# Windowed attention: softmax rows divided on GpSimd, transposed in place, one more stage between the steps

## The chip, the cores and the metric

One NeuronCore of a Trainium2 chip runs the whole program. The metric is the device time of one execution in microseconds (us), the median of several runs. Five engines work side by side, each through its own queue in order: TensorE (PE in the rows; PEld is its weight load), VectorE (DVE), ScalarE (ACT), GpSimd (POOL) and SyncE (SP), which issues the weight loads. Engines wait for each other through semaphores.

## The reference, cut to what matters

The program is two layers of a transformer-like block on 256 latent and 256 context tokens of width 1024. The change lies in the first layer, between the input projection and the output projection, where attention runs:

```python
def window_attention(q, k, v, k_ctx, v_ctx, sink):
    ...
    s_loc = jnp.where(valid[None, :, None, None], s_loc, NEG_INF)
    ...
    m = jnp.maximum(jnp.maximum(jnp.max(s_loc, axis=-1, keepdims=True),
                                jnp.max(s_ctx, axis=-1, keepdims=True)), s_sink)
    p_loc = jnp.exp(s_loc - m)
    p_ctx = jnp.exp(s_ctx - m)
    inv = 1.0 / (jnp.sum(p_loc, axis=-1, keepdims=True) + jnp.sum(p_ctx, axis=-1, keepdims=True)
                 + jnp.exp(s_sink - m))
    o = jnp.einsum('bnkgqs,bnskd->bnqkgd', (p_loc * inv).astype(v.dtype), vw) \
        + jnp.einsum('bnkgql,blkd->bnqkgd', (p_ctx * inv).astype(v.dtype), v_ctx)
```

`s_loc` and `s_ctx` are the scaled products of queries with keys, `valid` the band. There are 8 query heads and 2 key/value heads of width 64. Context queries read context keys only. The factor `inv` is one number per query row and head.

## The kernel before

All large products run in three passes of a split float format (`mm3`, L335 to L338): each fp32 operand is cut into a high part, cast by ScalarE (`wh`, L126), and a low part, subtracted by VectorE (`wl`, L127). A `Stream` object holds the weights in the order in which they are used: 1 MB units go through four raw buffers (`pump_dma`, issued on SP at L112), and `pump` cuts them in halves into four pairs of `wh`/`wl` buffers as these come free.

The program text gives each engine's instructions a priority by position. A planner of the framework then sets the order of each engine's queue by a model of durations, before anything runs. `issue_after` puts an instruction behind another one on the same engine.

The modulation vector of the layer is computed in 12 pieces (`ada_step(n)`): two 1 MB units, 16 small matmuls (`ada_mm`, L430), a copy, and one step later `ada_fin`: four transposes (L451), or, for pieces 4, 5, 10 and 11, products that spread a gate over 128 rows (L446, one for each of two streams) with a copy of each (L447).

Attention runs over 16 pairs (c, t): c counts four pairs of query heads, t four blocks of 128 queries. Blocks with t below 2 are latent (512 keys), the others context (256 keys). So four pairs, one value of c, are a period, with two long and two short pairs. For each pair j:

- `scores(j)`: for both heads a product with the high part of the keys (L929) and one with the low part (L932), and for long pairs a product that adds the mask from `CE` through the identity (L937, fp32). A pair takes two of the four `mm` banks of PSUM.
- `soft(j)`: VectorE row maxima (L947), the negative shift (L948), ScalarE exponentials with row sums (L953), the sink's term (L949, L956), the sum (L957) and its reciprocal (L958).
- `ptrans(j)`: TensorE turns the exponentials in blocks of 128 (L968) into the two `tr` banks, and ScalarE copies them out (L970).
- `av(j)`: the products with the values (L983) into one `po` bank, and products of the reciprocal, spread over 64 columns, with the identity (L987, fp32) into the other `po` bank. At the end of a period ScalarE copies that second bank (L992), VectorE multiplies (L993), and the result is cut into parts (L994, L995).

The loop at L999 issues `scores(j)`, `soft(j)`, `ptrans(j-1)`, `av(j-2)`, and between them `cut_q` (splitting the next query heads, L905, L906) and `sgu` (splitting the other half of the output projection's input, L916, L917). Weight splits for the output projection (`woe`) may be issued whenever buffers are free. After the loop the output projection uses all eight banks, then comes the residual, a norm (L564, L603) and the dense feed-forward layer, in which `Side` sums the second layer's modulation on VectorE (L498, L500).

## Time and profile before

| | us |
|---|---|
| median of 3 runs | 1601.19 (1600.59 to 1602.11) |
| the profiled execution, its own time | 1600.52 |
| its span in the trace | 1598.7 |
| PE busy | 1551.5 (97%) |
| DVE busy | 1286.8 (80%) |
| ACT busy | 981.1 (61%) |
| POOL busy | 0.2 (0%) |

The profile is one execution. Busy shares are averages over stages with different limits; matmuls overlap in the pipeline and their ends are modelled, so the time that a group of matmuls takes is best read from its start to the start of the next one.

### The profile page before, as it was taken

Reading aid. Unit: us, or ns where it says so; the run is one execution under the profiler, and the core shown is the slowest. Engines: PE = TensorE matmul, PEld = TensorE weight load, DVE = VectorE, ACT = ScalarE, POOL = GpSimd, SP = SyncE. Lnnn points to the kernel's source line nnn. Section 1 sums busy time; section 2 is a strip of 40 time slices with the busy share of each in tenths; the row PEclk is TensorE's granted clock in tenths of the full one; section 3 lists DMA queues with packets and bytes.
Section 4 is the critical chain, followed back from the end, with each engine's and each line's share of the span. In section 5 each row is a group of like instructions: output and inputs, shape, how many; then the busy total and the mean of one; then the engine's idle time right before and its main releaser. Section 6 shows DMA issues by size and latency. Waiting matters only on the chain.

```text
span 1598.7 us, 20230 instructions
## 1 busy us (share of the span) xinstructions
PE 1551.5 (97%) x7518; PEld 1237.4 (77%) x7518; DVE 1286.8 (80%) x1817; ACT 981.1 (61%) x1292; POOL 0.2 (0%) x4
## 2 busy tenths in 40 slices
PE   5999999999999999999999999999999999999996
PEld 3775787888888887776578888888888888888885
DVE  3577557475877576599899998998989899898987
ACT  4435625322222224679688877887778777877775
POOL 0000000000000000000000000000000000000000
PEclk9999999999999999999999999999999999999998
DMA  8867143444536441414699989999999999999980
GB/s 296 284 220 241 49 134 106 158 134 156 193 124 211 156 142 57 132 53 164 213 358 352 378 325 370 322 380 354 363 363 330 369 364 367 336 346 367 365 303 29
DMA packets 204267, 398.22 MB, mean 249 GB/s; under 512 B 7930, under 2 KB 66552, under 8 KB 204160
## 3 DMA queue, kind: packets, MB, share of 16 engines
q1 hardware_dynamic: 201184, 395.34, 69.7%
q10 hardware_dynamic: 2976, 1.50, 0.4%
q8 instruction: 61, 1.00, 0.3%
q14 instruction: 46, 0.38, 0.1%
HBM read 395.76 MB, written 1.05 MB: 248 GB/s over the span
## 4 chain that ended last, share of the span: by engine, by line
PE 87%; DVE 8%; ACT 2%; DMA 2%; issue 1%; ACTq 0%; DVEq 0%
PE mm L337 18%; PE mm L336 18%; PE mm L338 18%; PE po L337 8%; PE po L338 8%; PE po L336 8%; PE po L430 1%; PE tr L1441 1%; DVE wl L127 1%; PE po L983 1%; PE tr L1381 1%; PE tr L968 1%; DVE xn L500 1%; DMA raw<-in_w_in_e_dram 1%; DMA raw<-in_ada_w_o_dram 1%
## 5 line engine op out<-in xcount | busy, mean ns | idle before, releaser
L126 ACT CAST wh<-raw 128x1024 fp32r<-128x1024 f32 (+1 forms) x644 | 662.5, 1046 | 447.0 <-PE mm L337 145.4
L127 DVE TENSOR_TENSOR wl<-raw,wh 128x1024 fp32r<-128x1024 f32 (+1 forms) x644 | 759.4, 1214 | 127.5 <-ACT wh L126 115.9
L338 PE MATMUL mm<-wh,hLa 128*128 128x512 f32 (+1 forms) x800 | 299.2, 374 | 0.1
L337 PE MATMUL mm<-wl,xTH 128*128 128x512 f32 (+1 forms) x768 | 289.9, 377 | 0.0
L336 PE MATMUL mm<-wh,xTH 128*128 128x512 f32 (+1 forms) x768 | 287.3, 374 | 0.9 <-DVE xTH L1402 0.9
L336 PE MATMUL mm<-hH,wh 128*128 128x512 f32 (+1 forms) x608 | 228.7, 378 | 1.7 <-ACT gT L1148 1.5
L338 PE MATMUL mm<-hH,wl 128*128 128x512 f32 (+1 forms) x608 | 224.8, 371 | 0.5 <-DVE wl L127 0.5
L338 PEld LDWEIGHTS mm<-wh,hLa 128*128 128x128 f32 x800 | 150.9, 189 | 26.4 <-DVE hLa L1405 1.3
L337 PEld LDWEIGHTS mm<-wl,xTH 128*128 128x128 f32 x768 | 144.8, 189 | 27.1 <-DVE wl L127 3.0
L336 PEld LDWEIGHTS mm<-wh,xTH 128*128 128x128 f32 x768 | 144.8, 188 | 26.5 <-DVE xTH L1402 1.5
L337 PE MATMUL po<-wl,mg 128*128 128x512 f32 x352 | 137.4, 390 | 0.0
L338 PE MATMUL po<-wh,mg 128*128 128x512 f32 x352 | 136.4, 390 | 0.0
L336 PEld LDWEIGHTS mm<-hH,wh 128*128 128x128 f32 x608 | 114.2, 189 | 24.0 <-issue 2.0
L338 PEld LDWEIGHTS mm<-hH,wl 128*128 128x128 f32 x608 | 114.5, 188 | 20.1 <-DVE wl L127 0.7
L336 PE MATMUL po<-wh,mg 128*128 128x512 f32 x352 | 128.9, 391 | 0.0
L337 PE MATMUL mm<-hLb,wh 128*128 128x512 f32 (+1 forms) x304 | 112.9, 372 | 0.6 <-DVE hLb L616 0.6
L337 PE MATMUL mm<-hLa,wh 128*128 128x512 f32 (+1 forms) x304 | 112.8, 371 | 0.5 <-DVE hLa L616 0.5
L500 DVE SCALAR_TENSOR_TENSOR xn<-raw,act,xn 128x512 f32<-128x512 f32 x112 | 81.7, 747 | 1.2
L337 PEld LDWEIGHTS po<-wl,mg 128*128 128x128 f32 x352 | 66.2, 188 | 13.8 <-DVE wl L127 0.4
L336 PEld LDWEIGHTS po<-wh,mg 128*128 128x128 f32 x352 | 66.2, 188 | 13.5
L338 PEld LDWEIGHTS po<-wh,mg 128*128 128x128 f32 x352 | 66.0, 188 | 13.5
L337 PE MATMUL po<-wl,gH 128*128 128x512 f32 x176 | 69.9, 397 | 0.0
(392 smaller groups left out, 1873.9 us busy)
## 6 DMA issues: line engine op xcount, KB each, us to landing
raw<-in_moe_w_dram SPq DMA_DIRECT2D x264, 1024.0 KB
raw<-in_ffn_w_dram SPq DMA_DIRECT2D x33, 1024.0 KB
raw<-in_ada_w_e_dram SPq DMA_DIRECT2D x24, 1024.0 KB
raw<-in_ada_w_o_dram SPq DMA_DIRECT2D x24, 1024.0 KB
raw<-in_w_in_o_dram SPq DMA_DIRECT2D x10, 1024.0 KB
raw<-in_w_in_e_dram SPq DMA_DIRECT2D x7, 1024.0 KB
raw<-in_w_out_o_dram SPq DMA_DIRECT2D x5, 1024.0 KB
raw<-in_w_out_e_dram SPq DMA_DIRECT2D x2, 1024.0 KB
```

The lines of the kernel that those rows point to most:

```text
L126: sp = (self.nc.scalar.copy(hv, src), self.nc.vector.tensor_tensor(lv, src, hv.bitcast(F32), op=ALU.subtract))
L127: self.nc.vector.tensor_tensor(lv, src, hv.bitcast(F32), op=ALU.subtract))
L336: T.matmul(dst, aH, bH, start=start, stop=False)
L337: T.matmul(dst, aH, bL, start=False, stop=False)
L338: return T.matmul(dst, aL, bH, start=False, stop=stop)
L430: T.matmul(p[32 * g:32 * g + 32, :], act[:, 4 * u + g, :], w[:, g, :], start=(u == 0), stop=(u == 1))
L500: V.scalar_tensor_tensor(acc[s_], w[:, k, :], c, acc[s_], op0=ALU.mult, op1=ALU.add)
L968: T.transpose(p[:, P * b:P * b + P], pr[:, P * b:P * b + P], ident)
L983: T.matmul(ob[c][0][64 * i:64 * i + 64, P * t:P * t + P], vv[:, b, 64 * i:64 * i + 64], pts[i][:, P * jj:P * jj + P], start=(jj == 0), sto ...
L1381: T.matmul(p[:, 256 * j:256 * j + n], h[:, i, cs], dsp(i), start=(x == 0 and j == 0), stop=(x == 3 and j == 1))
L1441: T.transpose(p[:, P * j:P * j + P], s1[:, P * j:P * j + P], ident)
```

## The change

Each row of exponentials is multiplied by its reciprocal on GpSimd, in place, before it is transposed; the transposed blocks are copied back over the same tile; and the products that spread the reciprocal, and what follows them, are gone. `ptrans` and `av` of a pair come one iteration later (j-2 and j-3). The tag `pt` has eight buffers in place of six, and the query rotation's scratch tile is one of them. The mask and a copy of the identity are turned into the one-pass format by GpSimd, and the mask product uses them. Of the query splits, the copies of heads c = 1 to 3 move to GpSimd, and `sgu` moves to GpSimd whole. Pieces 8 and 9 of the modulation come after the query products, 10 and 11 in iterations 1 and 7; the units of piece 8 are loaded after the last query unit. Between piece 8 and the end of the loop, weights are split only in iterations 8, 10, 12 and 14, one half each.

```diff
         self.behind = None
+        self.hold = False

...

     def pump(self, n=None):
         self.pump_dma()
+        if self.hold and n is None:
+            return
         end = len(self.halves) if n is None else self.n_split + n
         while self.n_split < end:
             i, j = self.halves[self.n_split]
...
         ada_units("ae", we, n)
     for i, un in enumerate(e1_units):
         units.append(un)
-        for n in ((1, 3), (4,), (5,), (6,), (7,), (8,), (9, 10, 11), ())[i]:
+        for n in ((1, 3), (4,), (5,), (6,), (7,), (), (8, 9, 10, 11), ())[i]:
             ada_units("ae", we, n)
     units.append(kunit(("woe", 1), a["w_out_e"][0], 2, 2, 0, D))
     units += [woe_unit(u) for u in range(2)]
...
             pin.enter_context(tc.issue_after(last.ins))
             nc.scalar.dma_start(selb, a["shape_consts"][:, C_SELB:C_MASK])
             nc.scalar.dma_start(LT, a["shape_consts"][:, C_LT:C_SELB])
-            CE = sp.tile([P, C_ID - C_MASK], F32, name="CE")
-            nc.scalar.dma_start(CE, a["shape_consts"][:, C_MASK:C_ID])
-            cos, sin = CE[:, C_COS - C_MASK:C_COS - C_MASK + 256], CE[:, C_SIN - C_MASK:C_SIN - C_MASK + 256]
-            sw = sp.tile([P, 512], F32, tag="pt", bufs=6, name="sw").rearrange("p (g q) -> p g q", g=4)
+            CE = sp.tile([P, C_ID - C_COS], F32, name="CE")
+            nc.scalar.dma_start(CE, a["shape_consts"][:, C_COS:C_ID])
+            cos, sin = CE[:, 0:256], CE[:, 256:512]
+            mask = cpA.tile([P, 512], F32, tag="rtmp", bufs=2, name="mask")[:, 0:256]
+            nc.scalar.dma_start(mask, a["shape_consts"][:, C_MASK:C_COS])
+            masks = cpA.tile([P, 512], F32R, tag="rtmp", bufs=2, name="masks")
+            maskR, identR = masks[:, 0:256], masks[:, 256:384]
+            nc.gpsimd.tensor_copy(maskR, mask)
+            nc.gpsimd.tensor_copy(identR, ident)
+            sw = sp.tile([P, 512], F32, tag="pt", bufs=8, name="sw").rearrange("p (g q) -> p g q", g=4)
             nc.scalar.dma_start(sw, a["sgu_w"][0].rearrange("g p q -> p g q"))
             sb = sp.tile([P, 4, P], F32, tag="sb", name="sb")
             nc.scalar.dma_start(sb.rearrange("p g q -> p (g q)"), bcast_row(a["sgu_b"][0], 512))
...
                     for k in range(2):
                         mm3(pq[c], wH[:, k, cs], wL[:, k, cs], hH[:, 2 * u + k, :], hL[:, 2 * u + k, :],
                             u == 0 and k == 0, u == 3 and k == 1)
-                if u % 2 == 1:
-                    ada_step(8 + u // 2)
-            ada_fin(*pend.pop())
+            st.hold = True
+            for n in (8, 9):
+                ada_step(n)
             QS = [big("xn", [P, 4, 512], F32R), sp.tile([P, 4, 512], F32R, tag="vg", name="QS1")]
             qs = {}

             def rope_q(c):
-                qs[c] = ht() if c in (1, 2) else sp.tile([P, 512], F32, tag="pt", bufs=6, name=nm("q"))
+                qs[c] = ht() if c in (1, 2) else sp.tile([P, 512], F32, tag="pt", bufs=8, name=nm("q"))
                 rope(qs[c], pq[c])

             def cut_q(c):
                 q = qs.pop(c)
                 for i in range(2):
                     me, ot = slice(64 * i, 64 * i + 64), slice(64 - 64 * i, 128 - 64 * i)
-                    S.copy(QS[i][me, c], q[me, :])
+                    (S.copy if c == 0 else nc.gpsimd.tensor_copy)(QS[i][me, c], q[me, :])
                     V.tensor_tensor(QS[i][ot, c], q[me, :], QS[i][me, c].bitcast(F32), op=ALU.subtract)
             rope_q(0)
             cut_q(0)
             for c in range(1, 4):
                 rope_q(c)
-            ada_step(10)
-            pend.append(("ae", 11, ada_mm("ae", 11)))
             xH, xL = hH, hL

             def sgu(g):
-                S.copy(xH[:, g, :], uT[:, g, :])
-                V.tensor_tensor(xL[:, g, :], uT[:, g, :], xH[:, g, :].bitcast(F32), op=ALU.subtract)
+                nc.gpsimd.tensor_copy(xH[:, g, :], uT[:, g, :])
+                nc.gpsimd.tensor_tensor(xL[:, g, :], uT[:, g, :], xH[:, g, :].bitcast(F32), op=ALU.subtract)

             pairs = [(c, t) for c in range(4) for t in range(NT)]
-            sc_t, pr_t, ri_t, pt_t, ob = {}, {}, {}, {}, {}
+            last_n, sc_t, pr_t, ob = {}, {}, {}, {}

             def scores(j):

...
                 if t < 2:
                     off = P - P * t
                     for i in range(2):
-                        T.matmul(ps[i][:, off:off + P], ident, CE[:, P * t:P * t + P], start=False, stop=True)
+                        T.matmul(ps[i][:, off:off + P], identR, maskR[:, P * t:P * t + P], start=False, stop=True)
                 sc_t[j] = ps

             def soft(j):
...
                 V.tensor_tensor(snk, sk[:, :, c], neg, op=ALU.add)
                 prs = []
                 for i in range(2):
-                    pr = sp.tile([P, 512], F32, tag="pt", bufs=6, name=nm("pr"))
+                    pr = sp.tile([P, 512], F32, tag="pt", bufs=8, name=nm("pr"))
                     S.activation(pr[:, :n], ps[i][:, :n], AF.Exp, bias=neg[:, i:i + 1], scale=0.125,
                                  accum_out=sums[:, i:i + 1])
                     prs.append(pr)
                 S.activation(snk, snk, AF.Exp)
                 V.tensor_tensor(sums, sums, snk, op=ALU.add)
                 V.reciprocal(sums, sums)
+                for i in range(2):
+                    last_n[j] = nc.gpsimd.tensor_scalar(prs[i][:, :n], prs[i][:, :n], sums[:, i:i + 1], None, op0=ALU.mult)
                 pr_t[j] = prs
-                ri_t[j] = sums

             def ptrans(j):
+
                 nb = 4 if pairs[j][1] < 2 else 2
-                pts = []
-                for pr in pr_t.pop(j):
+                for pr in pr_t[j]:
                     p = tr()
                     for b in range(nb):
                         T.transpose(p[:, P * b:P * b + P], pr[:, P * b:P * b + P], ident)
-                    pt = sp.tile([P, 512], F32, tag="pt", bufs=6, name=nm("pt"))
-                    S.copy(pt[:, :P * nb], p[:, :P * nb])
-                    pts.append(pt)
-                pt_t[j] = pts
+                    S.copy(pr[:, :P * nb], p[:, :P * nb])

             def av(j):
                 c, t = pairs[j]
-                pts = pt_t.pop(j)
+                pts = pr_t.pop(j)
                 if c not in ob:
-                    ob[c] = po(), po()
+                    ob[c] = po()
                 blocks = range(4) if t < 2 else range(2, 4)
                 nb = len(blocks)
                 for jj, b in enumerate(blocks):
                     for i in range(2):
-                        T.matmul(ob[c][0][64 * i:64 * i + 64, P * t:P * t + P], vv[:, b, 64 * i:64 * i + 64],
+                        T.matmul(ob[c][64 * i:64 * i + 64, P * t:P * t + P], vv[:, b, 64 * i:64 * i + 64],
                                  pts[i][:, P * jj:P * jj + P], start=(jj == 0), stop=(jj == nb - 1))
-                ri = ri_t.pop(j)
-                for i in range(2):
-                    T.matmul(ob[c][1][64 * i:64 * i + 64, P * t:P * t + P], ri[:, i:i + 1].to_broadcast([P, 64]), ident,
-                             start=True, stop=True)
                 if t == NT - 1:
-                    o, r = ob.pop(c)
-                    q = sp.tile([P, 512], F32, tag="pt", bufs=6, name=nm("o"))
-                    S.copy(q, r)
-                    V.tensor_tensor(q, o, q, op=ALU.mult)
-                    last_o[0] = S.copy(xH[:, 4 + c, :], q)
-                    V.tensor_tensor(xL[:, 4 + c, :], q, xH[:, 4 + c, :].bitcast(F32), op=ALU.subtract)
+                    o = ob.pop(c)
+                    last_o[0] = S.copy(xH[:, 4 + c, :], o)
+                    V.tensor_tensor(xL[:, 4 + c, :], o, xH[:, 4 + c, :].bitcast(F32), op=ALU.subtract)

             NCB = len(pairs)
             last_o = [None]
-            for j in range(NCB + 2):
+            for j in range(NCB + 3):
                 if j < NCB:
                     scores(j)
                     soft(j)
-                if j % 4 == 1 and j < 12:
-                    cut_q(j // 4 + 1)
-                if 1 <= j <= NCB:
-                    ptrans(j - 1)
-                if 2 <= j:
-                    av(j - 2)
-                if j % 4 == 2 and j < NCB:
-                    sgu(j // 4)
+                if j == 1:
+                    cut_q(1)
+                if j in (4, 5):
+                    with tc.issue_after(last_n[j - 2].ins):
+                        cut_q(j - 2)
+                if j in (1, 7):
+                    ada_step(10 if j == 1 else 11)
+                if j in (7, 9, 11, 13):
+                    with tc.issue_after(last_n[j - 2].ins):
+                        sgu((j - 7) // 2)
+                if j in (8, 10, 12, 14):
+                    st.pump(1)
+                if 2 <= j < NCB + 2:
+                    ptrans(j - 2)
+                if 3 <= j:
+                    av(j - 3)
+            st.hold = False

             accs = {}
             order = [(t, h) for t in range(NT) for h in range(2)]
```

## Rows read from the trace of the kernel before

**Rows 1.** The page: busy time by engine; the chain that ended last, by engine.
```profile
PE 1551.5 (97%) x7518; PEld 1237.4 (77%) x7518; DVE 1286.8 (80%) x1817; ACT 981.1 (61%) x1292; POOL 0.2 (0%) x4
...
PE 87%; DVE 8%; ACT 2%; DMA 2%; issue 1%; ACTq 0%; DVEq 0%
```
**Rows 2.** Busy time by 10 us windows: length, engines (instructions), clock, DMA share, GB/s.
```profile
170.00:180.00 10.00, 10.00 (x87) 7.34 (x88) 6.12 (x21) 6.49 (x22) 0.00 (x0) 1.00 0.00 0
...
240.00:250.00 10.00, 8.21 (x36) 4.87 (x35) 9.86 (x27) 6.21 (x17) 0.00 (x0) 1.00 0.00 1
```
**Rows 3.** Timeline of PE, third attention period: start, us, engine, line, operation [idle before].
```profile
170.13 0.71 PE L937 MATMUL mm<-CE,ident 128*128 128x128 f32 x4
...
172.01 0.50 PE L929 MATMUL mm<-KH_kT,xn 128*128 128x512 f32 x1
...
173.11 0.71 PE L937 MATMUL mm<-CE,ident 128*128 128x128 f32 x4
173.75 0.44 PE L987 MATMUL po<-ident,ssum 128*64 128x128 f32 x4
174.12 0.39 PE L929 MATMUL mm<-KH_kT,xn 128*128 128x256 f32 x1
...
174.88 1.09 PE L968 MATMUL tr<-ident,pr 128*128 128x128 f32 x8
...
178.76 1.09 PE L983 MATMUL po<-pt,vv 128*64 128x128 f32 x16
179.69 0.61 PE L987 MATMUL po<-ident,ssum 128*64 128x128 f32 x8
180.22 0.50 PE L929 MATMUL mm<-KH_kT,xn 128*128 128x512 f32 x1
...
185.42 0.39 PE L987 MATMUL po<-ident,ssum 128*64 128x128 f32 x4
185.74 0.50 PE L929 MATMUL mm<-KH_kT,xn 128*128 128x512 f32 x1
```
**Rows 4.** Groups by line, 139.4 to 199.13 us: count, busy us, mean ns, idle before.
```profile
L987 PE MATMUL po<-ident,ssum 128*64 128x128 f32 x64 | 7.1, 278 | 0.1
...
L937 PE MATMUL mm<-CE,ident 128*128 128x128 f32 x32 | 6.0, 304 | 0.0
```
**Rows 5.** Timelines of DVE and ACT, softmax of the pair that ends rows 3's first line.
```profile
171.98 0.16 DVE L948 SCALAR_TENSOR_TENSOR sneg<-smx,nsk 128x2 f32<-128x2 f32 x1
...
174.92 0.15 DVE L958 RECIPROCAL ssum<-ssum 128x2 f32<-128x2 f32 x1
...
172.26 0.69 ACT L953 ACTIVATE pr<-mm,sneg 128x512 f32<-128x512 f32 x1 [3.10 <-DVE sneg L948]
```
**Rows 6.** Timelines of PE, ACT and DVE, first attention period: its limits and the weight splits.
```profile
139.40 0.50 PE L929 MATMUL mm<-KH_kT,xn 128*128 128x512 f32 x1
...
158.30 0.51 PE L929 MATMUL mm<-KH_swT,QS 128*128 128x512 f32 x1
...
148.56 2.02 ACT L126 CAST wh<-raw 128x1024 fp32r<-128x1024 f32 x2
...
153.28 2.35 DVE L127 TENSOR_TENSOR wl<-raw,wh 128x1024 fp32r<-128x1024 f32 x2
```
**Rows 7.** Groups by line, 139.4 to 199.13 us: elementwise work on tiles of 128x512.
```profile
L500 DVE SCALAR_TENSOR_TENSOR xn<-raw,act,xn 128x512 f32<-128x512 f32 x3 | 2.2, 743 | 0.0
...
L994 ACT CAST hH<-o 128x512 fp32r<-128x512 f32 x3 | 1.9, 633 | 0.5 <-DVE o L993 0.5
...
L498 DVE TENSOR_SCALAR xn<-raw,act 128x512 f32<-128x512 f32 x1 | 0.5, 478 | 0.0
```
**Rows 8.** Timeline of PE after the output projection: gate products, then the norm's transposes.
```profile
242.10 2.82 PE L446 MATMUL po<-adas,selb 99*128 99x512 f32 x6
...
244.98 1.02 PE L446 MATMUL po<-adas,selb 99*128 99x512 f32 x2
246.76 0.88 PE L564 MATMUL tr<-ident,vg 128*128 128x128 f32 x6 [0.75 <-DVE vg L603]
```

## What the change will do, predicted before it ran

> **What bounds the kernel now.** I read the page first: TensorE is busy 97% of the span, GpSimd not at all, and 87% of the chain that ended last is TensorE [rows 1]. A change can therefore only shorten the run where TensorE has less to do, or where it waits. Next I read the 10 us windows to find stages in which something else sets the pace. In the attention stage TensorE fills its window while VectorE and ScalarE are at 61% and 65% [rows 2]; after the output projection, at 240 to 250 us, VectorE is at 99% and TensorE has holes. Then the timeline of TensorE inside attention: from the second long pair of one period (172.01) to that of the next (185.74) it takes 13.73 us [rows 3], group against group with no idle entry in these rows. So a settled period is TensorE's own work, and what leaves its queue leaves the period. The first period is different: from 139.40 to 158.30 it takes 18.9 us [rows 6], with eight weight-split instructions on ScalarE and VectorE (four casts, four subtractions, two of each shown) in its middle. I counted the TensorE work of that stretch at the settled rates of rows 3 to about 16.6 us, the modulation piece in it included, so some 2.3 us are waiting. After the output projection everything that follows hangs on its end, so a gain or loss here moves the rest by the same amount.
>
> **The change, part by part.** The sum is made on the profiled execution's own 1600.52 us, which is 0.67 below the median of 1601.19; I add the sum to the median.
>
> *The reciprocal's products go.* These are 64 TensorE instructions [rows 4]; busy times overlap, so the price is read from start to next start. In the settled period they take 174.12 - 173.75 = 0.37, 180.22 - 179.69 = 0.53 and 185.74 - 185.42 = 0.32 [rows 3]: 1.22 us for 16. Times four periods is 4.9. The value products run at (179.69 - 178.76)/16 = 0.058 each; at that rate, with the switch between kinds of product staying, 64 cost 3.7. With the first period's looser groups it would be 5.8. I take -4.7 (-5.8 to -3.7). The copy, the multiplication and one bank that go with them lie off the path: both engines have a third of the window free.
>
> *The one-pass mask.* Each long pair runs four mask instructions in 173.75 - 173.11 = 0.64 us with the switch [rows 3], eight times, 32 in all [rows 4]. Two remain. The format's price at 128 columns is in no row; if a pass costs what it does now, half of some 0.55 goes, 2.2 in all. Nearest rows for one pass of 128 columns are 1.09/8 = 0.14 (transposes) and 0.93/16 = 0.06 (value products, 178.76 to 179.69). So -2.2 (-3.0 to -1.6).
>
> *Modulation.* Pieces 8 to 11 cost the same TensorE work wherever they stand. But the gate products of piece 10 move from behind the output projection, where TensorE has holes anyway, into the loop: two products of two passes, four instructions, at 1.02 per two [rows 8]: +1.9. In the old place TensorE waits for VectorE (0.75 us idle before the transposes, rows 8; VectorE 99%, rows 2), so leaving there earns little: -0.3 (-1.9 to 0). On SP the last query unit now passes piece 8's two units, and pieces 10 and 11 are loaded only once 8 and 9 are used, near 132 us; the first pairs' scores cover that. Output-projection weights queue behind them; they are wanted some 30 us later.
>
> *Splits held back.* The first period loses its split work on both engines (2.02 for a pair of casts, 2.35 for a pair of subtractions, rows 6, twice) and gets piece 10 as filler, but the pipeline is one stage deeper and fills later. Of the 2.3 us I count back -1.5 (-2.3 to 0). Four casts and subtractions now fall into later periods, where VectorE has about 39% free; each can hold the row maxima behind it for one subtraction, half of 2.35. With slack in two short pairs out of four I take +0.8 (0 to 3). The feed-forward loads that wait for these raw buffers start about 20 us later; they are covered by the 40 us output projection.
>
> *Rows divided on GpSimd.* The new wait. GpSimd does 32 multiplications in place, and between them six half-height query copies and eight `sgu` instructions, in one queue. Behind them wait the transposes, and behind those everything on TensorE. On VectorE the subtraction of `cut_q` now waits for a GpSimd copy, with the next row maxima queued behind it. No row shows GpSimd at work, so I bound one 128x512 multiplication, d, by other engines' rows for that shape: 0.48 on VectorE, 0.63 on ScalarE, 0.74 for a two-input operation [rows 7], and twice the last, 1.5, as upper end. I take 0.6 to 0.75, since no row hints at more and the operation has one tile input. Now the slack. For a long pair the chain from the end of its masks (170.13 + 0.71 = 170.84) over the shift (171.98) and the exponentials (172.26) to the end of the reciprocal (174.92 + 0.15 = 175.07) took 4.2 us [rows 3, 5]. The first head's rows come after d, the second's after 2d, wanted half a transpose group (0.55) later: 3.65 + 2d. TensorE passes two iterations in that time. For the second long pair, the worse case, these are two short scores, one long and one short transpose group, two short value groups: about 4.8 us (4.5 to 5.1, from the settled period less what was removed). So the wait is 2d - 1.15 per period: 0.1 at d = 0.63, 0.35 at 0.75. A wait there lets the next pairs catch up, so one counts per period: +1.0 in all (0 to 7.4, the end at d = 1.5).
>
> GpSimd's total stays below the period: 4d + 4(d/2) = 4.5 at d = 0.75, with `sgu` about 2 more, of some 12. [...]
>
> Sum: -4.7 - 2.2 + 1.9 - 0.3 - 1.5 + 0.8 + 1.0 = -5.0. On the median 1596.2; the profiled execution would read about 1595.5.
>
> **The rivals.**
>
> *All waits are hidden.* The planner places other TensorE work ahead of late transposes, as it does for `woe`. Then -4.7 - 2.2 + 1.9 - 0.3 - 2.3 = -7.6, 1593.6, and with the outer bounds 1590. For it: two short pairs of every four have over 2 us slack. Against: the queue is fixed before the run.
>
> *The shared way to memory.* VectorE's three small steps per pair with two tile operands (L948, L949, L957) and the 128x1024 subtractions meet GpSimd's reads. Two of the three lie on the chain; if each stands half a GpSimd operation, 0.37 us, the chain grows by 0.75 and the four periods by 3.0: 1599.2. For it: GpSimd is busy near half of the time. Against: no row of before can show it, since GpSimd is idle there. [...]
>
> *GpSimd is too slow, and the run ends later than before.* The gain without the wait is 6.0 us, 1.5 per period, so 2d - 1.15 = 1.5 gives the turning point, d = 1.3 us. At d = 1.5 the wait is 7.4 and the time 1602.6; with the 3.0 of the rival before, 1605.6. For it: nothing runs on GpSimd now, and its queue also carries two-input work. Against: 1.3 us is about twice any row of that shape with one input [rows 7].
>
> *The stage was not TensorE's after all:* the removed products only uncover the softmax chain. The period would stay near 13.7 and the time near 1600. Against: 61% and 65% on the other engines [rows 2].
>
> **How the numbers follow.** A measurement of this kernel can tell about 0.2%, 3.2 us, from no change, so faster means below 1598.0 and slower above 1604.4; the turning-point rival reaches beyond that only with both waits. Forecast (1594 to 1598) 0.40; all hidden (1590 to 1594) 0.20; shared memory or chain uncovered (1598 to 1602) 0.22; GpSimd too slow 0.18, of which 0.14 above 1604.4. Faster 0.60, same 0.26, slower 0.14. The range leaves out most of the last and the tail of the second: 1590 to 1605.
>
> **What would show it.** Right: the products of L987 gone; masks at about 0.3 us per pair; a settled period of 12 to 12.5 us, and the output projection's first long run starting near 194 in place of 199.13; GpSimd's 128x512 multiplication between 0.5 and 0.8. Wrong: idle entries on the transposes released by GpSimd, above 1 us per period; VectorE's L957 or L948 longer than 0.2 us; a first period still near 19 us; or the stretch from 240 to 260 growing because feed-forward loads came late.

## The result and the profile after

The changed kernel takes 1614.08 us (median; 1611.93 to 1615.45), the kernel before beside it 1600.89 (1599.89 to 1602.11): a ratio of 1.0075, 95% interval 1.0062 to 1.0087. It is 13.2 us **slower**; forecast were 5.0 us faster, and the range ended at 1605. Two executions of run 6 below took 1941.82 and 3142.94 us and stand apart from all others; its ratio leaves them out.

The profiled execution of after has a span of 1612.1 us. Its page, busy time by engine and the chain that ended last:

```profile
PE 1552.6 (96%) x7438; PEld 1235.4 (77%) x7438; DVE 1286.9 (80%) x1811; ACT 974.2 (60%) x1276; POOL 56.1 (3%) x52
...
PE 84%; DVE 8%; DMA 3%; ACT 2%; issue 1%; POOL 1%; ACTq 0%; POOLq 0%; DVEq 0%
```

Against [rows 1], TensorE runs 80 instructions fewer and is busy as long as before. GpSimd has 56.1 us of work where it had 0.2. It is busy for only 3% of the span, yet it stands in the chain with 1%, some 16 us.

To find the place I cut the span at five points of TensorE's timeline that both kernels have: the first modulation product, the transposes of `sw`, the first score product, the last product with v, and the first 128x512 product of the feed-forward part. Lengths in us:

| kernel | up to `sw` | `sw` to scores | attention loop | loop to feed-forward | the rest |
|---|---|---|---|---|---|
| before | 95.0 | 33.7 | 59.6 | 67.0 | 1332.8 |
| after | 97.3 | 29.3 | 74.6 | 65.9 | 1334.7 |
| difference | +2.3 | -4.4 | **+15.1** | -1.0 | +1.9 |

The second stretch has one modulation piece less (32 products of L433, where before has 48 of L430) and four 128x512 products less, hence the -4.4; the loop has one piece more (32 against 16) and the gate products of piece 10. The loop is where the time was lost. Its 10 us windows (columns as in [rows 2]):

```profile
160.00:170.00 10.00, 7.08 (x31) 2.87 (x30) 5.68 (x17) 6.06 (x19) 7.42 (x6) 0.83 0.11 34
...
180.00:190.00 10.00, 7.58 (x30) 4.65 (x31) 4.23 (x20) 5.47 (x19) 8.97 (x8) 0.73 0.42 147
190.00:200.00 10.00, 9.80 (x72) 6.58 (x70) 3.92 (x12) 5.02 (x14) 5.48 (x6) 0.76 0.00 0
```

TensorE has holes of up to 2.9 us in 10, GpSimd (fifth engine column) is busy 5.5 to 9 of 10, and the granted clock, 1.00 there before, is 0.83, 0.73 and 0.76. The timeline of TensorE shows both at work (last bracket: idle before, and what ended it):

```profile
161.60 0.66 PE L976 MATMUL tr<-ident,pr 128*128 128x128 f32 x4 [1.54 <-POOL pr L967]
163.64 0.78 PE L976 MATMUL tr<-ident,pr 128*128 128x128 f32 x4 [1.38 <-POOL pr L967]
...
176.21 0.50 PE L936 MATMUL mm<-KH_kT,xn 128*128 128x512 f32 x1
...
182.65 0.66 PE L976 MATMUL tr<-ident,pr 128*128 128x128 f32 x4 [1.53 <-POOL pr L967]
184.20 0.86 PE L976 MATMUL tr<-ident,pr 128*128 128x128 f32 x4 [0.89 <-POOL pr L967]
...
188.82 1.97 PE L976 MATMUL tr<-ident,pr 128*128 128x128 f32 x8
190.72 1.98 PE L988 MATMUL po<-pr,vv 128*64 128x128 f32 x16
...
195.89 0.50 PE L936 MATMUL mm<-KH_kT,xn 128*128 128x512 f32 x1
```

The transposes wait for GpSimd's rows, head by head, and 8 transposes then take 1.97 us against 1.09 in [rows 3]. From one second long pair to the next (176.21 to 195.89) the period is 19.7 us, where before it was 13.7. In the view of waits for the loop (total us, times, longest us), the transposes' weight load, their own line and the query copies:

```profile
PEld tr L976 <- POOL pr L967: 13.1, 14, 2.5
...
PE tr L976 <- POOL pr L967: 8.7, 9, 1.5
...
DVE xn L915 <- POOL xn L914: 3.7, 2, 2.7
```

And the groups of GpSimd and VectorE (count; busy us, mean ns; idle before):

```profile
L967 POOL TENSOR_SCALAR pr<-pr,ssum 128x512 f32<-128x512 f32 x16 | 25.3, 1599 | 19.4 <-DVE AB L472 8.4 <-DVE sneg L955 6.8 <-ACT pr L960 2.5
L967 POOL TENSOR_SCALAR pr<-pr,ssum 128x256 f32<-128x256 f32 x16 | 18.1, 1143 | 1.2 <-DVE ssum L965 0.9 <-PE tr L976 0.4
L924 POOL TENSOR_TENSOR hLa<-uT,hH 128x512 fp32r<-128x512 f32 x4 | 5.1, 1270 | 0.3
L923 POOL CAST hH<-uT 128x512 fp32r<-128x512 f32 x4 | 2.4, 611 | 0.0
...
L955 DVE SCALAR_TENSOR_TENSOR sneg<-smx,nsk 128x2 f32<-128x2 f32 x16 | 4.2, 262 | 0.2
L956 DVE TENSOR_TENSOR ssnk<-sk,sneg 128x2 f32<-128x2 f32 x16 | 4.2, 262 | 0.2
L964 DVE TENSOR_TENSOR ssum<-ssum,ssnk 128x2 f32<-128x2 f32 x16 | 3.7, 231 | 1.0 <-ACT ssnk L963 0.7 <-POOL pr L967 0.2
```

One division of rows takes 1.60 us at 128x512 in the mean, not 0.6 to 0.75. A copy of that shape on the same engine takes 0.61.

### The profile page after: what moved, and what is told of

Its sections match the earlier page's. It is cut to its first block, busy times and chain, and to the rows that moved or that the text cites. A ratio compares the mean times of both kernels' runs of the same rounds, so it can differ in the third digit from the quotient of the medians.

```text
span 1612.1 us, 20161 instructions
## 1 busy us (share of the span) xinstructions
PE 1552.6 (96%) x7438; PEld 1235.4 (77%) x7438; DVE 1286.9 (80%) x1811; ACT 974.2 (60%) x1276; POOL 56.1 (3%) x52
## 4 chain that ended last, share of the span: by engine, by line
PE 84%; DVE 8%; DMA 3%; ACT 2%; issue 1%; POOL 1%; ACTq 0%; POOLq 0%; DVEq 0%
PE mm L340 18%; PE mm L339 18%; PE mm L341 18%; PE po L340 8%; PE po L339 8%; PE po L341 8%; PE tr L1448 1%; PE po L433 1%; DVE wl L130 1%; POOL pr L967 1%; DMA raw<-in_w_in_e_dram 1%; DMA raw<-in_ada_w_e_dram 1%; PE tr L1388 1%; DVE xn L503 1%; DMA raw<-in_ada_w_o_dram 1%
## 5 line engine op out<-in xcount | busy, mean ns | idle before, releaser
L339 PEld LDWEIGHTS po<-wh,mg 128*128 128x128 f32 x352 | 66.1, 188 | 13.5
L341 PEld LDWEIGHTS po<-wh,mg 128*128 128x128 f32 x352 | 66.0, 188 | 13.5
```

The lines of the kernel that those rows point to most:

```text
L339: T.matmul(dst, aH, bH, start=start, stop=False)
L341: return T.matmul(dst, aL, bH, start=False, stop=stop)
```

## The experiments

**The theories.** The first is that the division on GpSimd is too long: the transposes wait for it, and the clock falls behind the waits. Its rivals: GpSimd is slow because other work shares its queue; GpSimd holds VectorE up (theory L); or the loss lies in the placement (modulation pieces, load order, held splits, deeper stages) and GpSimd only shows it. In each run below, the time before is that of the same chip.

**1. The rows on VectorE.** Everything else as changed.

```diff
-                    last_n[j] = nc.gpsimd.tensor_scalar(prs[i][:, :n], prs[i][:, :n], sums[:, i:i + 1], None, op0=ALU.mult)
+                    last_n[j] = V.tensor_scalar(prs[i][:, :n], prs[i][:, :n], sums[:, i:i + 1], None, op0=ALU.mult)
```

> The changed kernel with one edit: the 32 in-place row divisions run on VectorE instead of GpSimd; query copies and the sgu split stay on GpSimd. Theory R (a row division takes 1.6 us on GpSimd for 128x512 where 1.3 was the turning point, and TensorE waits for it at the transposes): the waits on GpSimd at the transposes go, the division takes about 0.5 us, and the time falls to 1593 to 1598, below the kernel before by 3 to 8 us. Theory P (what costs is where modulation pieces and weight splits now stand, and the loads that come later for it): the time stays above 1606. Theory L (VectorE is blocked by whatever GpSimd does): sgu and query copies still run there, so part of the loss stays, 1599 to 1604.

Measured: 1600.09, ratio 0.9993 (0.9983 to 1.0003). One word of code takes back the whole loss, 14 us against after by the medians. The time lies in the range of theory L (1599 to 1604), not in that of R (1593 to 1598), and P is out. The loop is 65.0 us. No transposes wait any more, but a clock of 0.92 and 0.74 stands in the windows from 170 to 190, behind an idle entry of 0.34 us for ScalarE.

**2. GpSimd with nothing in the loop.** As 1, and the query copies and `sgu` back on ScalarE and VectorE.

```diff
-                    (S.copy if c == 0 else nc.gpsimd.tensor_copy)(QS[i][me, c], q[me, :])
+                    S.copy(QS[i][me, c], q[me, :])
-                nc.gpsimd.tensor_copy(xH[:, g, :], uT[:, g, :])
-                nc.gpsimd.tensor_tensor(xL[:, g, :], uT[:, g, :], xH[:, g, :].bitcast(F32), op=ALU.subtract)
+                S.copy(xH[:, g, :], uT[:, g, :])
+                V.tensor_tensor(xL[:, g, :], uT[:, g, :], xH[:, g, :].bitcast(F32), op=ALU.subtract)
```

> As the run before, and the query copies go back to ScalarE and the sgu split to ScalarE and VectorE: GpSimd does nothing in the attention loop. Theory R: within 2 us of the run before, since those operations were never waited for by TensorE. Theory L: faster than the run before by 2 to 5 us, since VectorE's steps with two tile inputs are no longer blocked. Theory P: still above 1606.

Measured: 1598.51, ratio 0.9981 (0.9971 to 0.9991); loop 61.1 us, granted clock 1.00 through it. Its windows:

```profile
170.00:180.00 10.00, 9.70 (x80) 6.70 (x79) 8.75 (x28) 6.72 (x22) 0.00 (x0) 1.00 0.14 40
180.00:190.00 10.00, 9.28 (x74) 6.45 (x72) 9.26 (x29) 7.30 (x23) 0.00 (x0) 1.00 0.19 66
```

VectorE, at 6.1 in [rows 2], is now busy 8.8 and 9.3 of 10. The period from second long pair to second long pair (169.09 to 183.03, no modulation work inside) is 13.9 us, not 12 to 12.5. I read this as VectorE setting the pace once the products are gone; TensorE is itself busy 9.7 and 9.3 of 10 there, so it is argued and not shown alone. By the medians the run is 1.6 us below run 1: within R's 2, short of L's 2 to 5.

**3. GpSimd with the rows alone.** The diff of 2 on the changed kernel; the rows stay on GpSimd.

> The changed kernel with GpSimd keeping the row divisions alone; query copies and sgu split go back to ScalarE and VectorE. Theory R with the duration alone as cause: still 1607 to 1614, with waits of 1 to 1.5 us at the transposes of the first halves. If the queue in front of the divisions (about 12 us of copies and splits) is what makes them late: 1600 to 1605.

Measured: 1611.46, ratio 1.0065 (1.0043 to 1.0086); loop 69.2 us, with 7.6 us of waits for GpSimd left, as theory R expected. Taking the other work off the queue is worth 2.6 us by the medians and 1.6 by the ratios, with intervals that overlap (four executions each); in the two profiles the loops differ by 5.4. The rows alone keep most of the loss.

**4. GpSimd busy, and nobody waits.** As 2, with the same 32 multiplications on a tile that nobody reads.

```diff
+                    nc.gpsimd.tensor_scalar(idle_t[:, :n], idle_t[:, :n], sums[:, i:i + 1], None, op0=ALU.mult)
```

> Row divisions on VectorE, query copies and sgu split on ScalarE and VectorE, and GpSimd does the same 32 multiplications on a tile that nobody reads, released by the same reciprocals. It is the kernel without GpSimd work plus a busy GpSimd that nobody waits for. Theory R: as fast as the kernel without GpSimd work, within 1.5 us. Theory L (the shared way to memory): VectorE's small steps grow from 0.15 to 0.5 us and more, and the time rises by 3 to 8 us over that kernel.

Measured: 1599.25, ratio 0.9996 (0.9981 to 1.001), 0.7 us above run 2 by the medians and 2.4 by the ratios, with intervals that overlap. VectorE's groups of this run (the division, then the two small steps):

```profile
L969 DVE TENSOR_SCALAR pr<-pr,ssum 128x512 f32<-128x512 f32 x16 | 9.3, 622 | 0.0
...
L957 DVE SCALAR_TENSOR_TENSOR sneg<-smx,nsk 128x2 f32<-128x2 f32 x16 | 4.3, 267 | 0.1
L966 DVE TENSOR_TENSOR ssum<-ssum,ssnk 128x2 f32<-128x2 f32 x16 | 3.5, 218 | 0.9 <-ACT ssnk L965 0.8
```

In run 2 these were 476, 152 and 153 ns. So these steps of VectorE are longer while GpSimd is busy. What that costs while nobody waits for GpSimd is not sharp here: by the two intervals, anything from nothing to some 5 us. The small steps did not grow to the 0.5 us of theory L.

**5. The mask alone** on the kernel before, from its one load (masks and unit matrix copied once on GpSimd).

```diff
-                        T.matmul(ps[i][:, off:off + P], ident, CE[:, P * t:P * t + P], start=False, stop=True)
+                        T.matmul(ps[i][:, off:off + P], identR, maskR[:, P * t:P * t + P], start=False, stop=True)
```

> The kernel before with nothing changed but the one-pass mask (the mask and the unit matrix are copied once, and the 16 masked matmuls at the scores run in one pass). By the sum on record the mask is worth 2.2 us, all of it on TensorE's path: 1598.7, with the long run of the output projection about 2 us earlier than in the kernel before (199.13) and no wait longer. If TensorE's time between two evictions is slack that the steps on the other engines fill (the settled period is set by VectorE and ScalarE and not by TensorE), the mask gives back less than 0.5 us: 1600.5 to 1601.

Measured: 1599.76, ratio 0.9989 (0.998 to 0.9998). TensorE's timeline of this run:

```profile
153.68 0.44 PE L972 MATMUL tr<-ident,pr 128*128 128x128 f32 x2 [0.45 <-ACT pt L974]
...
154.78 1.92 PE L987 MATMUL po<-pt,vv 128*64 128x128 f32 x14
156.62 0.80 PE L933 MATMUL mm<-KH_kT,xn 128*128 128x512 f32 x1
...
173.79 0.44 PE L941 MATMUL mm<-masks 128*128 128x128 f32 x2
174.16 0.44 PE L991 MATMUL po<-ident,ssum 128*64 128x128 f32 x4
```

The masks take 0.37 us with the switch, 0.27 less than the 0.64 of [rows 3], so 2.2 for eight pairs, as forecast. At 154 TensorE is 0.33 us ahead of before, waits 0.45 for ScalarE where before waited 0.28, and then 14 value products take 1.92 us (1.09 before) and a score 0.80 (0.50). The granted clock is 0.83 in the window from 150 to 160; it was 1.00. At 167 TensorE is 0.9 behind, and the later pairs only win that back: the last product with v ends at 198.96, before at 198.98. The second half of the expectation (slack that swallows the gain) did not hold as put: in this execution the masks' gain was there, and a fall of the clock took it. It was the slowest of eleven (1601.01); the median is 1.2 us below before.

**6. The placement alone** on the kernel before.

```diff
-        for n in ((1, 3), (4,), (5,), (6,), (7,), (8,), (9, 10, 11), ())[i]:
+        for n in ((1, 3), (4,), (5,), (6,), (7,), (), (8, 9, 10, 11), ())[i]:
...
+                if j in (1, 7):
+                    ada_step(10 if j == 1 else 11)
+                if j in (8, 10, 12, 14):
+                    st.pump(1)
```

> The kernel before with the placement alone: modulation pieces 8 and 9 behind the q products, 10 and 11 inside the attention loop, the order of the loads that belongs to it, and the weight splits held back to four set blocks. By the sum on record it is worth +1.9 - 0.3 - 1.5 + 0.8 = +0.9: 1601.5 to 1602.5. If the reordered load and its early split are what holds the kernel without GpSimd work back (its q products ended 2 us later than its instructions need), this run shows the same: q products that end 1 to 2 us later than before less the two pieces moved out, waits on the modulation pieces' transfers, and a time of 1602.5 to 1605. If the placement relieves the first period as forecast and costs nothing upstream: 1599 to 1600.5.

Measured: 1598.02, ratio 0.9979 (0.997 to 0.9989), 3 us faster where +0.9 was forecast, and below all three ranges. The stretch from `sw` to the scores is 4.4 us shorter, the loop 61.1 us, 1.5 longer, although it took in a piece and the gate products (four instructions, 1.98 us at 162.61). The moved work filled waits and was nearly free; it is not the cause of the loss.

**7. The arithmetic alone, rows on VectorE, near and far stages.** The kernel before with the division ahead of the transposes, eviction in place, no broadcast of the reciprocals and the one-pass mask with its own load; placement as before. Near: transposes one pair behind the scores. Far: two, as in the change.

```diff
-                if 1 <= j <= NCB:
-                    ptrans(j - 1)
-                if 2 <= j:
-                    av(j - 2)
+                if 2 <= j < NCB + 2:
+                    ptrans(j - 2)
+                if 3 <= j:
+                    av(j - 3)
```

> The kernel before with the arithmetic of the change alone: rows divided before the transposes, on VectorE; transposes evicted in place; no matmuls that broadcast the reciprocals; the one-pass mask. Placement, load order and stage distance stay those of the kernel before, and GpSimd has no work in the loop. TensorE loses 4.7 + 2.2 = 6.9 us by the sum on record. VectorE gains 16 x (0.48 + 0.48) + 16 x (0.35 + 0.35) over the loop less the four evictions. If those sums hold and VectorE has room: 1594 to 1596. If the division stands in the chain from the sums to the transposes with only one period between (a period of near stages): each period gets a wait of 0.3 to 1 us before its transposes and the time is 1597 to 1602. If the upstream reorder is what held the version without GpSimd work at 1598.5: this one is at least 1.5 us below that.

> As the run with the arithmetic alone on VectorE, with the stages of the change: transposes two periods and the products with v three periods behind the scores. One more drain period at the end, of transposes and products only, costs nothing by itself since the same instructions run. If the distance hides the division that near stages expose: faster than the near one by 1 to 3 us, 1594 to 1597. If VectorE's busy time and not the distance sets the period: within 0.5 us of the near one. If it is the placement that cost the version without GpSimd work its gain: 1.5 us or more below its 1598.5.

Measured: near 1605.27, ratio 1.0029 (1.0016 to 1.0041), loop 65.6 us; far 1603.29, ratio 1.0006 (0.9993 to 1.0019), loop 59.5. Both missed the times that the sum on record gave (1594 to 1597). The near one shows what one wait costs:

```profile
176.63 1.90 PE L978 MATMUL tr<-ident,pr 128*128 128x128 f32 x8 [1.15 <-DVE pr L969]
...
181.27 1.94 PE L978 MATMUL tr<-ident,pr 128*128 128x128 f32 x8
```

After 1.15 us of idle time, the transposes take 1.90 and 1.94 us; the granted clock was 0.83, 0.82 and 0.69 in the windows from 170 to 200 (a second wait, of 1.67 us for ScalarE, ends at 193.26). Without the placement the arithmetic gains nothing in the median, with either distance. But of the far version's twelve executions three, with a mean granted clock of 0.992 and 0.993, took 1596.7 to 1597.9 us; the other nine, at 0.986 to 0.989, took 1601.5 to 1605.6.

**8. Placement and mask together**, with the masks from the one load.

> The kernel before with the placement (pieces 8 to 11, load order, held splits) and the one-pass mask together, and nothing else of the change: no division ahead of the transposes, the reciprocals still broadcast by matmuls. The placement alone gave 1598.0 and the mask alone 1599.8. If what was lost of the mask's 2.2 us in its own run was one fall of the granted clock behind a wait for ScalarE in the first period, and the moved modulation pieces fill that period: 1595.5 to 1597. If a shorter TensorE always ends in such a wait somewhere in the loop: 1597.5 to 1598.5, with a window of the loop at a granted clock under 0.9.

Measured: 1597.77, ratio 0.9975 (0.9966 to 0.9985), no clear step from the placement alone. The time lies in the second range, without the low clock that was to go with it: in its profile the loop is 59.8 us at full clock, 1.3 less than in run 6.

**9. The mask's load behind the late rows**, else run 2.

```diff
-            nc.scalar.dma_start(mask, a["shape_consts"][:, C_MASK:C_COS])
...
             late_rows()
+            nc.scalar.dma_start(mask, a["shape_consts"][:, C_MASK:C_COS])
```

> The version with no work on GpSimd in the loop (rows divided on VectorE, 1598.5), with the mask's own load issued behind all the late rows instead of ahead of them. If that small load ahead of the others is what makes the stretch up to the gate's transposes longer (98.7 us from the first modulation matmul to the transposes of sw, 95.0 in the kernel before, 96.6 with the placement alone): that stretch falls to about 96.6 and the time to 1596 to 1597. If it is the load order of the units or the larger ring of buffers: nothing changes, 1598 to 1599.

Measured: 1596.53, ratio 0.9972 (0.9962 to 0.9983). Time and stretch are as expected of the load: the stretch up to `sw` is 96.2 us in place of 98.7. Over all runs: with the mask as a load of its own ahead of the rows that stretch is 96.4 to 99.4 us (ten profiles, mean 98.0), with it behind them 95.7 to 97.2 (four, mean 96.4), with the load undivided 95.0 to 96.6 (four, mean 95.7). So the separate load costs about 1.6 us in the profiles. The times confirm it only weakly: the intervals of runs 2 and 9 overlap.

**10. Half of the rows on GpSimd.** As run 2, the second head of each pair on GpSimd.

```diff
+                    last_n[j] = (V if i == 0 else nc.gpsimd).tensor_scalar(prs[i][:, :n], prs[i][:, :n], sums[:, i:i + 1], None, op0=ALU.mult)
```

> The version with no work on GpSimd in the loop, with one of the two row divisions of each pair on GpSimd and the other on VectorE. GpSimd then has 8 x 1.6 + 8 x 1.14 = 22 us of work in a loop of about 61 us, where the change gives it 44 us of rows. If the length of the division against the period decides (both of a pair in 3.2 us against a pair's share of the period of about 3.4 us, behind the chain of soft): the waits of the transposes on GpSimd nearly go, the loop is 61 to 63 us, and the time 1597 to 1600. If any division on GpSimd in the chain costs by its latency: waits of about half those of the change, a loop of 65 to 69 us, and 1603 to 1606.

Measured: 1596.80, ratio 0.9966 (0.9954 to 0.9978); loop 59.1 us. GpSimd's division is longer than in the change (1.82 us in the mean at 128x512), but a pair asks it for one, and one wait of 0.40 us is left; loop and time lie a little below the first range. One division per pair on GpSimd in the chain shows no cost here (loop 61.1 us in run 2, with none there); two in a row did show one (69.2 in run 3).

**11. The price by itself.** As run 2, with 16 instructions on a tile that nobody reads. They were meant to run behind the loop and ran from 72.6 to 95.5 us; VectorE was busy for 12.7 of the 25 us from 70 to 95, 4.5 of them in the last five.

> The version with no work on GpSimd in the loop, and behind the loop, while VectorE has little to do, 16 instructions on GpSimd on a tile of 128 rows by 512 that nobody reads: four multiplications by a scalar of each row, four by a constant, four copies, four with two tiles as inputs. It gives the price of the division by itself. If 1.6 us is what such an instruction takes alone: the first four take 1.5 to 1.6 us each, and the copies 0.6 to 0.9. If it was VectorE at the shared port that stretched it from the 0.6 to 0.75 of the sum on record: 0.6 to 0.9 for all forms of one input.

Measured, GpSimd's groups, and the spread of the first form (minimum, median, maximum):

```profile
L1022 POOL TENSOR_SCALAR gq<-gq,sk 128x512 f32<-128x512 f32 x4 | 8.3, 2080 | 4.8 <-DMA sk<-in_attn_sink_dram 4.5
L1024 POOL TENSOR_SCALAR gq<-gq 128x512 f32<-128x512 f32 x4 | 6.8, 1691 | 0.3
L1028 POOL TENSOR_TENSOR gq<-gq 128x512 f32<-128x512 f32 x4 | 4.2, 1040 | 0.3
L1026 POOL COPY gq<-gq 128x512 f32<-128x512 f32 x4 | 2.4, 612 | 0.2
```

```profile
L1022 POOL TENSOR_SCALAR gq<-gq,sk x4: 1562/1564/3628, 72.6 to 79.6; 128x512 f32<-128x512 f32 x4
```

The form that the change uses takes 1.56 us (one of 3.63 lifts the mean), the form with a constant 1.49 (one of 2.30 does the same). The expectation of 1.5 to 1.6 held for three of four, and the shortest took 1.562: no sign of something shorter that VectorE stretched. The form with two inputs (here the same tile twice), which looks dearer, takes 1.04. The two long ones are those beside VectorE's subtractions of two tiles (GpSimd's and VectorE's timelines):

```profile
72.58 3.63 POOL L1022 TENSOR_SCALAR gq<-gq,sk 128x512 f32<-128x512 f32 x1 [4.49 <-DMA sk<-in_attn_sink_dram]
...
72.49 2.36 DVE L130 TENSOR_TENSOR wl<-raw,wh 128x1024 fp32r<-128x1024 f32 x2
...
84.14 2.78 DVE L130 TENSOR_TENSOR wl<-raw,wh 128x1024 fp32r<-128x1024 f32 x2 [4.90 <-ACT wh L129]
```

The constant form's long one ran from 84.42 to 86.72. So GpSimd's instructions were longer beside VectorE's as well: 3.63 against 1.56 us, 2.30 against 1.49.

**12. The length alone.** The changed kernel, each division as a multiplication of two inputs.

```diff
-                    last_n[j] = nc.gpsimd.tensor_scalar(prs[i][:, :n], prs[i][:, :n], sums[:, i:i + 1], None, op0=ALU.mult)
+                    last_n[j] = nc.gpsimd.tensor_tensor(prs[i][:, :n], prs[i][:, :n], sums[:, i:i + 1].to_broadcast([P, n]), op=ALU.mult)
```

> The changed kernel with each row division written as a GpSimd multiplication of two inputs, the second being the reciprocal broadcast along the row, and nothing else altered: the same 32 divisions on the same engine. Measured by itself that form took 1.04 us at 128x512 against 2.08 for the form with a scalar of each row. If the duration against the turning point of 1.3 us decides: the waits of the transposes on GpSimd fall from 21.8 us to under 6, the loop from 74.6 to 60 to 64 us, and the time from 1614 to 1598 to 1602. If it is the engine's latency or its queue, not the duration: at least half the waits stay and the time is 1606 or more.

Measured: 1604.47, ratio 1.0017 (1.0007 to 1.0026), 9.6 us below after. The same engine, queue and place; the groups, TensorE's timeline and the waits:

```profile
L967 POOL TENSOR_TENSOR pr<-pr,ssum 128x512 f32<-128x512 f32 x16 | 16.3, 1039 | 21.9 <-DVE AB L472 8.4 <-DVE sneg L955 7.2 <-DVE ssum L965 4.3
```

```profile
178.15 0.66 PE L976 MATMUL tr<-ident,pr 128*128 128x128 f32 x4 [0.84 <-POOL pr L967]
179.15 1.12 PE L976 MATMUL tr<-ident,pr 128*128 128x128 f32 x4 [0.34 <-POOL pr L967]
```

```profile
PEld tr L976 <- POOL pr L967: 6.3, 10, 1.9
...
PE tr L976 <- POOL pr L967: 3.1, 6, 1.0
```

TensorE's idle time behind GpSimd falls from 8.7 to 3.1 us and the loop from 74.6 to 67.6. The 2.08 of the expectation is the mean that the one of 3.63 lifts, and its 21.8 counts the weight loads too, 13.1 + 8.7; here it is 9.4, not under 6, and less than half. Loop and time are above what was expected of the duration (60 to 64 and 1598 to 1602, the time by 2.5), and the time is below the rival's 1606: waits are left, and after two of them (0.84 and 0.34 at 178 and 179) the granted clock is 0.55 in the window from 180 to 190.

**13. Combinations with the late mask load.** All rows in the two-input form with GpSimd's other work taken off; and half of them on GpSimd in either form.

> All row divisions on GpSimd in the form of two inputs, with the copies and the gate's splits back on ScalarE and VectorE (GpSimd has the divisions alone) and the mask's load behind the late rows. If 1.04 us each is short enough, GpSimd takes 16 x 0.48 + 16 x 0.35 = 13 us off VectorE, which was busy 8 to 9.8 of 10 us in the loop without GpSimd: 1593 to 1596. If both inputs' reads stretch VectorE's own steps and its chain is what the loop waits for: 1597 to 1600.

> One of the two row divisions of each pair on GpSimd, the other on VectorE, as in the run that gave 1596.8, and the mask's load behind the late rows, as in the run that gave 1596.5 (both against 1601.6 before); no other work on GpSimd in the loop. If the two gains are of different stretches (the loop, and the stretch up to the transposes of sw) they add: 1594 to 1595.5. If the medians of those two runs differ from 1598.5 by the spread of runs alone: 1596.5 to 1598.

> As the run with half the divisions on GpSimd and the late mask, with GpSimd's half in the form of two inputs. GpSimd has 16 x about 1 us in a loop of 60 us. Within 1 us of the run with half in the dearer form if no transposes wait for GpSimd any more (0.4 us of such a wait was left there): 1594 to 1596. Slower than that by 1 us or more if the form of two inputs stretches VectorE's steps.

Measured: all rows 1598.53, ratio 0.9987 (0.9978 to 0.9997), with 3.3 us of waits for GpSimd left and the clock at 1.00; half, dearer form, 1597.52, ratio 0.9971 (0.9962 to 0.9979); half, two inputs, 1597.33, ratio 0.9971 (0.9959 to 0.9982). The gains of runs 9 and 10 did not add, and the first range missed in all three (1593 to 1596, 1594 to 1595.5, 1594 to 1596). Half on GpSimd is no better than none (run 9). Runs 8, 9, 10 and the two halves here, 1596.5 to 1597.8, beat both kernels by their intervals, by less than half a per cent, and are not told apart among themselves.

The half with the dearer form had a profile worth reading. Its loop took 65.8 us, in run 10, with the same loop, 59.1. TensorE's timeline and windows:

```profile
140.62 1.76 PE L433 MATMUL po<-raw,act 128*32 128x512 f32 x8 [1.17 <-DMA raw<-in_ada_w_e_dram]
```

```profile
140.00:150.00 10.00, 9.38 (x36) 4.64 (x36) 5.58 (x25) 3.88 (x12) 3.67 (x2) 0.54 1.04 397
150.00:160.00 10.00, 10.00 (x60) 5.84 (x59) 6.08 (x17) 5.37 (x18) 2.25 (x2) 0.77 0.10 40
```

One wait of 1.17 us for a modulation piece's load (0.17 in run 10), and the clock is 0.54 and 0.77 for 20 us. This one execution lost some 6 us by it; the median did not.

## Why the prediction was wrong

**The step that failed** is "Rows divided on GpSimd", by its size. I took d as 0.6 to 0.75 us "since no row hints at more and the operation has one tile input", with 1.5 as upper end; it measured 1.60 in the kernel and 1.56 alone, beyond even that end. What it did to the time: TensorE waited 8.7 us behind GpSimd where the sum had 1.0. VectorE's and ScalarE's rows of the same shape, 0.48 to 0.74 us [rows 7], were no bound for GpSimd. "GpSimd's total stays below the period" fell with it: GpSimd is busy for 53.9 us between 140 and 210, some 13.5 per period, where 12 to 12.5 were forecast.

**The kind of wait held, its place did not.** The formula of the wait, 2d - 1.15 per period, gives 2.05 at d = 1.6, 8.2 for four periods; TensorE's idle entries behind GpSimd sum to 8.7. At d = 1.04 (run 12) it gives 3.7; they sum to 3.1. That the wait grows with d is shown: from after to run 12 the third period's two entries go from 1.53 and 0.89 to 0.84 and 0.34, 1.24 in all, near twice the 0.56 that the division lost. But the sums agree in part by luck. The 1.15 was worked out for the second long pair, as the worse case; in the trace the long waits of the last three periods stand at the first long pair (161.60 and 163.64, 182.65 and 184.20, 200.59 and 202.14). For the third period's first long pair, masks on TensorE, reciprocal on VectorE and first division on GpSimd:

```profile
173.90 0.44 PE L944 MATMUL mm<-masks 128*128 128x128 f32 x2
...
180.67 0.17 DVE L965 RECIPROCAL ssum<-ssum 128x2 f32<-128x2 f32 x1
...
181.03 6.20 POOL L967 TENSOR_SCALAR pr<-pr,ssum 128x512 f32<-128x512 f32 x4 [1.64 <-PE po L988]
```

From the end of the masks to the end of the reciprocal this is 6.5 us, where I had put 4.2; ScalarE's exponentials began at 178.34, 1.6 us after the shift that they need, behind the copy of an earlier pair's transposes. The turning point of 1.3 us is not confirmed as a number: at 1.04 run 12 is still 0.2% slower than before, while run 13 with the same form, nothing else in the queue and the late mask load gains 0.1%; at 1.60 both kernels with all rows there lose. So the rival "GpSimd is too slow" is what happened. Its price, 1602.6 to 1605.6, was short.

**What the price left out: the granted clock.** I wrote that a wait "lets the next pairs catch up". In place of that, the granted clock was lower behind the waits: 0.83 in the window from 160 to 170, 0.73 and 0.76 in those from 180 to 200. From 184.20 to 192.62 TensorE's groups took 8.4 us; at the durations of the same groups at full clock (a short score 0.75, a long score 1.10, 8 transposes 1.02, 16 value products 0.93, 4 transposes 0.59) they take 4.4. That is 4.0 lost in one place, and the three windows together bound the loss at 0.17 + 0.27 + 0.24 of 10 us each, 6.8. Waits of 8.7 and some 6 for the clock are about the loop's +15.1. The rest cancels, by an estimate from the timelines: the 6.9 taken off TensorE, against some 4.3 for the piece and the gate products that came in, 1.4 for more waits on loads and ScalarE, and 1.2 for five more products of the output projection. Runs 5, 7 (near) and 13 (half, dearer form) show the same sequence after waits for ScalarE (0.45 us, then 0.83), VectorE (1.15, then 0.83, 0.82 and 0.69) and a load (1.17, then 0.54 and 0.77).

Not every wait is followed by it. Run 3 has two of 1.18 and 1.38 us with the granted clock at 1.00 in their window and the next (TensorE's timeline and the window):

```profile
162.10 0.66 PE L976 MATMUL tr<-ident,pr 128*128 128x128 f32 x4 [1.18 <-POOL pr L967]
164.13 0.66 PE L976 MATMUL tr<-ident,pr 128*128 128x128 f32 x4 [1.38 <-POOL pr L967]
...
160.00:170.00 10.00, 7.44 (x40) 2.99 (x39) 5.32 (x16) 4.78 (x16) 7.19 (x4) 1.00 0.17 41
```

**The gain without the wait**, -6.0 in my sum, was -3.0 in run 2 and -4.5 in run 9 by their ratios, and its parts were wrong in both directions. The products of L987 are gone and the masks take the time forecast, -6.9 of TensorE's work; with the rows on VectorE little of that is seen. From `sw` to the end of the loop run 2 and run 6 (placement alone) both take 90.4 us, but run 2 has twelve products of the output projection in its loop and run 6 three; from `sw` to the feed-forward start they take 156.0 and 157.6, and run 8, with the mask and the products of L987, takes 155.9. My case against the rival "the stage was not TensorE's after all" was that VectorE stood at 61% [rows 2]. That share holds before the change; the division alone adds 16 x (0.476 + 0.346), 13.2 us, to the loop's VectorE, and 6.1 became 8.8 to 9.3. The period stayed at 13.9, near the 13.7 of that rival, though with a division on VectorE that the change does not have there. The placement, forecast at +0.9, gave -3: the loop took in some 4.3 us of products and grew by 1.5, so there was more to fill than the 2.3 us that I counted.

**The other points.** That VectorE is held up shows: L955 and L964 take 262 and 231 ns in the mean, over the 0.2 us that I had named, against 156 and 155 before. Run 4 agrees (267 and 218 against 152 and 153 in run 2), and run 11 has it the other way round, GpSimd's 3.63 us beside VectorE's subtractions. That the cause is a shared way to memory, or a shared port, was a guess of mine; the runs show the lengths alone. Not every step with two tile inputs grew: in run 4 L958 takes 158 ns, in run 2 the same step 149. The price is 0.7 us by the medians of runs 2 and 4 and 2.4 by the ratios. The other work in the queue of GpSimd's divisions cost 2.6 us by the medians (run 3). VectorE waited 3.7 us for the query copies; what that was worth by itself I did not separate from the 2.6. The output projection's first long run starts at 211.39, not near 194. The stretch behind it did not grow (loop to feed-forward 65.9 us against 67.0), so the late loads were covered, as forecast; those of piece 10 were not covered by the first pairs' scores: TensorE waited 0.76 and 0.48 us for them, at 140.41 and 142.98. Missed was the split of the load of masks and tables, about 1.6 us before `sw` (run 9).

**Open.** Behind the feed-forward start after is 1.9 us longer than before and run 3 as well, the other runs not; I did not trace it. That the clock falls because of the waits is the order seen in after and in runs 5, 7, 12 and 13, not a separate test, and the waits alone do not settle it: run 3 above, and run 13 with all rows (waits of up to 0.88) and with half in two inputs (1.00 for a load), kept 1.00. In run 7 far the executions of one program differ by 9 us, with their mean clock. Runs 1 and 2 differ by their clock, 0.74 against 1.00, after waits of 0.34 and 0.20 us, so how long a wait has to be, and what else it takes, is not settled here.

## What to carry to other kernels

Before work goes to an engine that is idle in the trace, measure that very instruction on that engine: another engine's row for the same shape was no bound here (0.48 us on VectorE, 1.56 on GpSimd), and the form mattered more than the number of inputs (1.56 us with a scalar of each row, 1.04 with a second tile). Where a feeder has two pieces per pair, one of them could go to the idle engine at no cost that showed (1596.80 us in run 10), where both of them lost (1611.46 in run 3); it gained nothing clear over giving it none (runs 9 and 13). And price a new wait on TensorE with the clock that may fall behind it: beside 8.7 us of waits, up to 6.8 went with the clock.

## What the hardware showed that I had not expected

- On GpSimd, at 128x512, a multiplication by a scalar of each row takes 1.56 us, by a constant 1.49, by a second tile 1.04, a copy 0.61. Beside VectorE's subtractions of two tiles one of the first took 3.63 and one of the second 2.30 (run 11).
- A wait on TensorE of 1.17 us (run 13) was followed by two 10 us windows with a granted clock of 0.54 and 0.77; in the two profiles of the same loop, 59.1 and 65.8 us. Waits of 1.18 and 1.38 us in run 3 were not.
- With GpSimd busy beside it (run 4 against run 2), VectorE's steps of 0.15 us on two columns took 0.15 to 0.27 in the mean (one of them 1.13, in after), and a division of 0.48 took 0.62.
